# HGRN2 decays in a hybrid diffusion backbone: running products of the gates in place of exponentials of summed logarithms

## The chip, the cores and the metric

The kernel runs on one core of one Trainium2 chip. The metric is device time in microseconds (us) of one execution; the median of three runs is given, lower is better. Matmuls run on TensorE (PE; its weight loads are PEld), elementwise work on VectorE (DVE), ScalarE (ACT) and GpSimd (POOL); SyncE (SP) starts the transfers. Each engine works off its own instructions in a fixed order and waits on semaphores for the others.

## What is computed

Two layers, each a mixer with four head groups (HGRN2, SSD, RG-LRU, retention; all in both directions) and a ConvFFN. One sample, 256 context and 512 latent tokens, 1024 features, float32. The part that changes is the HGRN2 group: four heads of 128 channels, two directions, a gate per token and channel.

```python
log_f = jnp.logaddexp(jnp.log(jnp.maximum(lb_s, LB_FLOOR)), jnp.log1p(-lb_s) + jax.nn.log_sigmoid(u))
k_a = (1.0 - lb_s) * jax.nn.sigmoid(-u)
...
def step(S, inp):          # gla_chunk_scan, one chunk of tokens
    b = jnp.cumsum(lc, axis=1)
    rel = masked_decay(mask, b[:, :, None] - b[:, None, :])
    scores = jnp.sum(qc[:, :, None] * kc[:, None] * rel, axis=-1)
    y = (jnp.einsum("btsh,bshv->bthv", scores, vc)
         + jnp.einsum("bthk,bhkv->bthv", qc * jnp.exp(b), S))
    b_last = b[:, -1]
    S = (jnp.exp(b_last)[..., None] * S
         + jnp.einsum("bshk,bshv->bhkv", kc * jnp.exp(b_last[:, None] - b), vc))
```

The score of a query at t and a key at s is weighted, channel by channel, with the product of the gates between them.

## The kernel before

Every projection is a float32 product made of three matmuls with split operands (`proj_T`, line 303, columns on the partitions; `proj_N`, line 320, tokens on the partitions). A unit of weights `wr` comes by DMA; `Weights` (line 287 and 288) splits it: ACT casts the high part `wh`, then DVE makes the low part `wl` as a difference. A group of 24 matmuls fills one PSUM tile `pp` (there are three), which ACT or DVE empties.

Beside the projections run the mixers of the head groups, in the order `C0 C1 A0 A1 BC B0 B1 D0 D1` (A is HGRN2; the digit is a half of 256 channels, two heads). `interleave` (line 1291) emits steps of both by estimated times, and a scheduler, which models durations of its own, then sets each engine's order. Casts and evacuations carry a high priority there, so that what stands in an engine's row ahead of a cast is what the scheduler thought would be over in time.

HGRN2 works on chunks of 128 tokens, six of them, in two parts of three (`p`; in layer 1 part 0 scores only one chunk).

- `prepA` (line 547), once per half: sigmoids on ACT (556, 557), gate bounds on DVE (561 to 564), two logarithms per head and direction on ACT (568, 569), their sum on POOL (573), and a scan on DVE that sums the logs along each chunk (574). The result stays in `E`.
- `mixA_head` (line 583), once per head: scores at eight levels. Level -1 takes equal tokens; level `lev` takes pairs of adjacent blocks of m = 2^lev tokens, and weights both sides with the decay to the border between the blocks. For each level and part DVE and POOL take differences of the sums (657 to 660), ACT takes their exponential `g` (661), DVE and POOL multiply queries and keys with it into `lv` (664, 667), and PE makes the block products (672), which DVE merges under a mask (678). Every level starts again from `E`, so levels do not depend on one another.
- Beside the levels, `states` takes keys decayed to the chunk's end (595 to 601), whose products with the values go through `state_chain`; lines 690 to 695 make queries decayed from the chunk's start, and line 705 adds all up.

## Time and profile before

| | |
|---|---|
| device time, median of 3 runs | 2704.52 us |
| lowest, highest | 2702.71, 2708.85 us |
| profiled execution: span from first to last instruction | 2706.8 us |
| instructions in it | 42271 |
| mean granted TensorE clock | 0.967 |
| DVE, ACT, POOL busy | 1810.4, 1138.2, 1027.8 us |

For the profiled execution no device time of its own is listed beside the span; the span lies 2.3 us above the median and inside the range of the three runs. Busy times of different engines overlap, so they do not add up to the span. A matmul's length in the trace is its stay in a pipeline; the pace is the distance between starts.

### The profile page before, as it was taken

What the parts mean: (1) busy time and instruction counts of PE and PEld (TensorE: products, weight loads), DVE (VectorE), ACT (ScalarE), POOL (GpSimd) and SP (SyncE); (2) the same over time, 40 slices, a digit from 0 to 9 for tenths busy, and PEclk for the clock granted to TensorE, in tenths of its full rate; (3) what the DMA queues carried; (4) which work ended last, traced back from release to release, by engine and by line L of the source; (5) the groups of instructions that cost most, each with busy time, mean ns of one, the idle gap of its engine ahead of it and who ended that gap; (6) DMA issues with size and microseconds to landing.
All of it is one profiled execution on the core that took longest, in us unless ns stands there. A gap on an engine that the chain in (4) does not pass through costs nothing.

```text
span 2706.8 us, 42271 instructions
## 1 busy us (share of the span) xinstructions
PE 2512.5 (93%) x15910; PEld 2175.9 (80%) x15910; DVE 1810.4 (67%) x3573; ACT 1138.2 (42%) x2118; POOL 1027.8 (38%) x1327
## 2 busy tenths in 40 slices
PE   6878989998999989999999989799989999899997
PEld 4877888888997877878888878687789987788885
DVE  3898879887674673434344677988887767644457
ACT  3864464532332153322322267656442342543332
POOL 0346736366341760000001574564646436400006
PEclk9989999999999999999999989899999999899999
DMA  7134421233265264442222422212132264323333
GB/s 256 52 111 153 132 75 55 64 121 98 65 210 174 72 194 149 139 133 79 63 63 74 129 87 61 73 54 85 33 115 77 82 222 136 110 91 97 97 113 106
DMA packets 201596, 291.08 MB, mean 108 GB/s; under 512 B 15568, under 2 KB 145200, under 8 KB 201392
## 3 DMA queue, kind: packets, MB, share of 16 engines
q1 hardware_dynamic: 201392, 288.37, 34.3%
q8 instruction: 126, 2.06, 0.3%
q14 instruction: 78, 0.64, 0.1%
HBM read 256.73 MB, written 31.59 MB: 107 GB/s over the span
## 4 chain that ended last, share of the span: by engine, by line
PE 55%; DVE 24%; POOL 7%; DMA 6%; issue 4%; ACT 3%; SPq 0%; DVEq 0%; POOLq 0%; ACTq 0%
PE pp L313 25%; PE pp L1201 13%; PE pp L330 8%; DVE wl L288 3%; PE pp L1245 2%; DVE lv__t L664 1%; DVE g__t L658 1%; DVE g__t L657 1%; DVE lv__t L667 1%; PE ada__pm L383 1%; DVE E__t L574 1%; POOL S__t L1223 1%; DMA aB__t<-rowsd 1%; POOL aff__t L1281 1%; POOL aff__t L1282 1%
## 5 line engine op out<-in xcount | busy, mean ns | idle before, releaser
L313 PE MATMUL pp<-uh,wl 128*128 128x512 f32 (+2 forms) x1952 | 684.5, 351 | 21.4 <-DVE wl L288 13.7
L313 PE MATMUL pp<-ul,wh 128*128 128x512 f32 (+2 forms) x1952 | 681.5, 350 | 15.3 <-DVE ul L499 15.3
L313 PE MATMUL pp<-uh,wh 128*128 128x512 f32 (+2 forms) x1952 | 676.5, 347 | 0.0
L288 DVE TENSOR_TENSOR wl<-wr,wh 128x512 fp32r<-128x512 f32 (+1 forms) x552 | 432.9, 798 | 163.7 <-ACT wh L287 163.0
L287 ACT CAST wh<-wr 128x512 fp32r<-128x512 f32 (+1 forms) x552 | 337.2, 621 | 454.5 <-PE pp L1201 216.6
L313 PEld LDWEIGHTS pp<-uh,wl 128*128 128x128 f32 x1952 | 376.4, 193 | 69.2 <-DVE wl L288 15.2
L313 PEld LDWEIGHTS pp<-ul,wh 128*128 128x128 f32 x1952 | 377.1, 193 | 62.4 <-DVE ul L499 18.1
L313 PEld LDWEIGHTS pp<-uh,wh 128*128 128x128 f32 x1952 | 377.0, 193 | 42.2 <-issue 4.5
L330 PE MATMUL pp<-wl,uh 128*128 128x256 f32 (+1 forms) x1216 | 357.5, 294 | 16.3 <-DVE wl L288 16.2
L330 PE MATMUL pp<-wh,ul 128*128 128x256 f32 (+1 forms) x1216 | 361.1, 297 | 5.4 <-DVE gst__t L1416 3.3
L330 PE MATMUL pp<-wh,uh 128*128 128x256 f32 (+1 forms) x1216 | 353.1, 291 | 0.0
L330 PEld LDWEIGHTS pp<-wl,uh 128*128 128x128 f32 x1216 | 236.1, 194 | 21.5 <-DVE wl L288 17.3
L893 POOL MEMSET padF__t<- 128x1 f32 x44 | 4.3, 97 | 654.2 <-DVE gt__t L909 286.4
L330 PEld LDWEIGHTS pp<-wh,ul 128*128 128x128 f32 x1216 | 235.7, 194 | 10.1 <-DVE gst__t L1416 4.2
L330 PEld LDWEIGHTS pp<-wh,uh 128*128 128x128 f32 x1216 | 236.1, 194 | 1.5 <-issue 0.4
L1201 PE MATMUL pp<-wh,ccl__t 128*128 128x512 f32 x440 | 173.5, 398 | 2.1 <-DVE gst__t L1416 2.1
L1201 PE MATMUL pp<-wh,cch__t 128*128 128x512 f32 x440 | 174.0, 396 | 0.0
L1201 PE MATMUL pp<-wl,cch__t 128*128 128x512 f32 x440 | 173.7, 395 | 0.0
L1210 DVE TENSOR_TENSOR S__t<-pp,S__t 128x384 f32<-128x384 f32 (+1 forms) x240 | 89.7, 417 | 124.0 <-PE pp L1201 123.4
L909 DVE SCALAR_TENSOR_TENSOR cva__t<-padF__t,PT,cva__t 128x769 f32<-128x769 f32 (+1 forms) x44 | 42.0, 954 | 136.2 <-ACT cva__t L905 136.0
L1218 POOL TENSOR_TENSOR S__t<-S__t,bc__t 128x384 f32<-128x384 f32 (+1 forms) x60 | 60.2, 1016 | 172.0 <-DVE S__t L1210 170.1
L661 ACT ACTIVATE g__t<-g__t 128x768 f32<-128x768 f32 (+1 forms) x112 | 81.2, 736 | 93.4 <-DVE g__t L658 51.0
(359 smaller groups left out, 4911.4 us busy)
## 6 DMA issues: line engine op xcount, KB each, us to landing
wr<-w_in_dram SPq DMA_DIRECT2D x112, 512.0 KB, 4.0
wr<-ffn_w_in_dram SPq DMA_DIRECT2D x88, 512.0 KB, 3.6
wr<-ada_w_dram SPq DMA_DIRECT2D x80, 512.0 KB, 4.2
wr<-ffn_w_out_dram SPq DMA_DIRECT2D x44, 512.0 KB, 3.8
wr<-w_out_dram SPq DMA_DIRECT2D x32, 512.0 KB, 5.0
aB__t<-rowsd SPq DMA_DIRECT2D x40, 256.0 KB, 3.9
adw__t<-ada_w_dram SPq DMA_DIRECT2D x32, 256.0 KB, 5.3
hres<-aff__t SPq DMA_DIRECT2D x32, 192.0 KB, 1.9
```

The source lines that it names most:

```text
L287: A.copy(hi[:, :m], rq)
L288: V.tensor_tensor(out=lo[:, :m], in0=rq, in1=hi[:, :m].bitcast(F32), op=SUB)
L313: PE.matmul(ps[:, :t1 - t0], a[:, cs], b[k // 4][:, k % 4, t0:t1], start=n == 0, stop=n == 23)
L330: PE.matmul(ps[:, :nn], a[k // 4][:, k % 4, ts], b, start=n == 0, stop=n == 23)
L383: PE.matmul(ps[32 * (j0 + j):32 * (j0 + j) + 32, :256], condT[:, k, :], raw[x][:, j * 256:(j + 1) * 256], start=k == 0, stop=k == 7)
L574: V.tensor_tensor_scan(out=e, data0=st["scan"], data1=e, initial=0.0, op0=MULT, op1=ADD)
L661: A.activation(g[:, :2 * N], g[:, :2 * N], AF.Exp)
L909: V.scalar_tensor_tensor(out=o[:, lo:hi], in0=pad[:, lo + j:hi + j], scalar=w(j), in1=acc[:, lo:hi], op0=MULT, op1=ADD)
L1201: PE.matmul(ps, a[:, ts], b, start=n == 0, stop=n == 3 * kt - 1)
L1210: V.tensor_tensor(out=o, in0=src, in1=o, op=ADD)
L1218: G.tensor_tensor(out=o, in0=o, in1=gcols(r, lo, hi), op=MULT)
L1245: PE.matmul(ps, a[:, ts], b, start=n == 0, stop=n == 3 * kt - 1)
```

## The change

The gates themselves are kept, no logarithms. For each head and part one tile `f2` holds the gates of both directions, `k2` the keys of both. `prepA` keeps the sigmoids and the bounds (line 564, 565 of the changed kernel) and loses the logarithms, their sum, the scan and the scan's constant. In `mixA_head`, queries `Q` start as q times the gate (`begin`, line 629); at each level `scores` gathers the keys of both directions by an ACT copy into `kl` (595), or takes the tiles as they are at level 6, and lets the queries be read with strides by PE (609). Then `grow` makes the next level in place: POOL multiplies the half of the keys that lie ahead of a border with the product of the gates of the neighbouring block (643), DVE does the same to the queries (646) and halves the table of block products `tot` (649). After level 6, keys and queries are decayed over the whole chunk, and `states` and the output take them as they are. Both parts of a head now go through the levels together. Comments also go, and with them line numbers move.

```diff
 def projA(l, u, hf, dtr, st):
-        E = [[t3(f"E{d}{h}") for h in range(2)] for d in range(2)]
+        f2 = {(h, p): t3(f"f{h}{p}") for h in range(2) for p in range(2)}
...
-                A.copy(v3(E[d][ct], 129)[:, t0 // 128:t1 // 128, 1:129], v3(ps[:, :t1 - t0], 128))
+                A.copy(f2[ct, t0 // PW][:, d * PW:(d + 1) * PW], ps[:, :t1 - t0])
...
 def prepA(st, prm):
-            V.tensor_scalar(out=E1[x], in0=E1[x], scalar1=c1, scalar2=fl, op0=MULT, op1=ADD)
-            V.tensor_scalar(out=v3(l2[x], 128), in0=E1[x], scalar1=2.0 ** 60, scalar2=1.0, op0=MULT, op1=MIN)
-            V.tensor_scalar(out=E1[x], in0=E1[x], scalar1=2.0 ** -60, scalar2=None, op0=MAX)
-            V.tensor_scalar(out=k[x][:, :768], in0=k[x][:, :768], scalar1=c1, scalar2=None, op0=MULT)
...
-                A.activation(l2[x], l2[x], AF.Ln)
-                last = A.activation(E1[x], E1[x], AF.Ln)
...
-            G.tensor_tensor(out=E1[x], in0=E1[x], in1=v3(l2[x], 128), op=ADD)
-            V.tensor_tensor_scan(out=e, data0=st["scan"], data1=e, initial=0.0, op0=MULT, op1=ADD)
+                f, k = st["f2"][h, p][:, ds], st["k2"][h, p][:, ds]
+                V.tensor_scalar(out=f, in0=f, scalar1=c1, scalar2=fl, op0=MULT, op1=ADD)
+                V.tensor_scalar(out=k, in0=k, scalar1=c1, scalar2=None, op0=MULT)
...
 def mixA_head(st, prm, y, h):
...
+            elif lev < 6:
+                ks = t3("kl")
+                A.copy(ks[:, :N], strided(K[p], chs[p][0] % 3 * 128, [[2 * m, N // (2 * m)], [PW + m, 2], [1, m]]))
...
+                    elif lev < 6:
+                        ql = strided(Q[p], qc, [[2 * m, 32 // m], [N + m, 2], [1, m]])
+                    else:
+                        kl = K[p][:, hs * PW + kc:hs * PW + kc + 64]
+                        qo = j * 128 + 64 + N if hs == 0 else j * 128
+                        ql = Q[p][:, qo:qo + 64]
+                    PE.matmul(sc[64 * hs:64 * hs + 64, j * 64:(j + 1) * 64], kl, ql, start=True, stop=True)
...
+        def begin(p):
+            V.tensor_tensor(out=v3(Q[p][:, :2 * N], N), in0=q[:, None, t0:t0 + N].to_broadcast([128, 2, N]),
+                            in1=strided(f, fo + PW, [[-PW, 2], [1, N]]), op=MULT)
+        def grow(p, lev):
...
+            G.tensor_tensor(out=strided(K[p], 0, [[2 * m, nk], [PW + m, 2], [1, m]]),
+                            in0=strided(K[p], 0, [[2 * m, nk], [PW + m, 2], [1, m]]),
+                            in1=strided(t, off + 1, [[2, nk], [step - 1, 2], [0, m]]), op=MULT)
+            V.tensor_tensor(out=strided(Q[p], 0, [[2 * m, nq], [N + m, 2], [1, m]]),
+                            in0=strided(Q[p], 0, [[2 * m, nq], [N + m, 2], [1, m]]),
+                            in1=strided(t, off + step + b0 + 1, [[2, nq], [-step - 1, 2], [0, m]]), op=MULT)
+            V.tensor_tensor(out=strided(tn, noff, [[nk, 2], [1, nk]]), in0=strided(t, off, [[step, 2], [2, nk]]),
+                            in1=strided(t, off + 1, [[step, 2], [2, nk]]), op=MULT)
+            tot[p] = (tn, noff, nk)
...
+        for lev in range(-1, 7):
+            for p in range(2):
+                if lev == 0:
+                    begin(p)
+                scores(p, lev)
+                if lev >= 0:
+                    grow(p, lev)
+                yield 1.8
+        for p in range(2):
+            states(p)
+            yield 2.0
```

`strided(t, off, dims)` is a view of a tile from column `off` on, with a step and a count for each dimension. The tile of 774 columns holds forward data in columns 0 to 383 and backward data in 384 to 767, so at m = 1 the pattern of `grow` goes back and forth between the two with every element.

The change moves instructions on all engines; the orders below show three places. ACT, layer 0, second half, around the evacuations of the query projection, before (`E` the summed logs, `dec` and `kt` the exponentials for the states, `q` the queries that leave PSUM):

```order
L591 ACTIVATE decA__ss_4098<-E__t_2732 128x6
L597 ACTIVATE kt__t_4101<-kt__t_4101 128x384
L533 COPY q__t_3782<-pp 128x384
L591 ACTIVATE decA__ss_4098<-E__t_2734 128x6
L598 ACTIVATE kt__t_4101<-E__t_2734 128x384
L591 ACTIVATE decA__ss_4773<-E__t_2733 128x6
L533 COPY q__t_3783<-pp 128x384
L287 CAST wh<-wr 128x512
```

Each exponential that reads `E` comes after a scan of line 574, and the cast of the next weights stands behind it. In the changed kernel ACT has, a little earlier in the same half:

```order
L530 COPY f__t_2693<-pp 128x384
L556 ACTIVATE k__t_3691<-f__t_2693 128x768
L557 ACTIVATE f__t_2693<-f__t_2693 128x768
L595 COPY kl__t_3874<-k__t_3690 128x384
L595 COPY kl__t_3860<-k__t_3691 128x384
L595 COPY kl__t_3927<-k__t_3690 128x384
L595 COPY kl__t_3887<-k__t_3691 128x384
L530 COPY f__t_2694<-pp 128x384
L595 COPY kl__t_3953<-k__t_3690 128x384
L556 ACTIVATE k__t_3692<-f__t_2694 128x768
L284 CAST wh<-wr 128x512
```

No scan and no logarithm is left ahead of a cast; copies of keys, each behind a growth step on POOL, stand there now. The same in layer 0, first half, around the four evacuations of the queries, changed kernel:

```order
L535 COPY q__t_1718<-pp 128x384
L284 CAST wh<-wr 128x512
L595 COPY kl__t_2133<-k__t_1870 128x384
L595 COPY kl__t_2181<-k__t_1871 128x384
L595 COPY kl__t_2194<-k__t_1870 128x384
L535 COPY q__t_1718<-pp 128x384
L595 COPY kl__t_2243<-k__t_1871 128x384
L595 COPY kl__t_2256<-k__t_1870 128x384
L535 COPY q__t_1719<-pp 128x384
L595 COPY kl__t_2328<-k__t_1871 128x384
L284 CAST wh<-wr 128x512
L595 COPY kl__t_2341<-k__t_1870 128x384
```

The fourth evacuation comes right behind. Between the first and the fourth PE passes three groups of 24 matmuls, and ACT seven copies. POOL, layer 0, second half, before and then in the changed kernel (`ks` are the keys of level -1):

```order
L643 TENSOR_TENSOR ks__t_4089<-k__t_3910,k__t_3911 128x384
L505 TENSOR_TENSOR rs__ss_3674<-rs__ss_3674,pw 128x3
L573 TENSOR_TENSOR E__t_2732<-E__t_2732,l__t_3914 128x6x128
L573 TENSOR_TENSOR E__t_2734<-E__t_2734,l__t_3915 128x6x128
L659 TENSOR_TENSOR g__t_4108<-E__t_2732 128x192
L573 TENSOR_TENSOR E__t_2733<-E__t_2733,l__t_3916 128x6x128
L659 TENSOR_TENSOR g__t_4148<-E__t_2732 128x96x2
```

```order
L590 TENSOR_TENSOR ks__t_3795<-k__t_3690 128x384
L643 TENSOR_TENSOR k__t_3690<-k__t_3690,f__t_2692 128x192x2
L590 TENSOR_TENSOR ks__t_3805<-k__t_3691 128x384
L643 TENSOR_TENSOR k__t_3690<-k__t_3690,tot__t_3826 128x96x2x2
L643 TENSOR_TENSOR k__t_3691<-k__t_3691,f__t_2693 128x192x2
L643 TENSOR_TENSOR k__t_3690<-k__t_3690,tot__t_3826 128x48x2x4
L502 TENSOR_TENSOR rs__ss_3376<-rs__ss_3376,pw 128x3
```

Three instructions on a quarter of the data per level have become one on all 768 columns, each behind the one before it on the same tile. PE's matmuls are the same in number and shape in both orders.

## Rows read from the trace of the kernel before

**Rows 1.** The page, part 1: busy us (share of the span) xinstructions.

```profile
PE 2512.5 (93%) x15910; PEld 2175.9 (80%) x15910; DVE 1810.4 (67%) x3573; ACT 1138.2 (42%) x2118; POOL 1027.8 (38%) x1327
```

**Rows 2.** Windows: stretch, length, busy PE PEld DVE ACT POOL, clock, DMA, GB/s.

```profile
150.00:545.00 395.00, 360.35 (x2887) 319.95 (x2886) 342.31 (x615) 209.62 (x382) 219.35 (x282) 0.94 0.33 103
1690.00:2005.00 315.00, 278.38 (x1975) 243.38 (x1974) 272.68 (x567) 175.90 (x349) 175.23 (x275) 0.95 0.22 65
```

**Rows 3.** Waits of PE, whole span: who waited for whom, us in total, times, longest.

```profile
PE sc__pm L672 <- DVE lv__t L667: 18.1, 12, 4.0
...
PE pp L330 <- DVE wl L288: 16.2, 4, 8.7
...
PE pp L313 <- DVE wl L288: 13.7, 5, 7.4
```

**Rows 4.** Timeline, layer 0, first half: start, length, instruction [idle before <-releaser].

```profile
192.95 1.58 ACT L569 ACTIVATE E__t<-E__t 128x768 f32<-128x768 f32 x2 [3.50 <-DVE E__t L563]
...
194.44 0.61 ACT L287 CAST wh<-wr 128x512 fp32r<-128x512 f32 x1
...
198.38 0.94 DVE L288 TENSOR_TENSOR wl<-wr,wh 128x512 fp32r<-128x512 f32 x1
...
199.35 0.34 SPq L377 DMA_DIRECT2D wr<-ada_w_dram  x1
...
203.32 1.08 PE L383 MATMUL ada__pm<-wr,condT 128*32 128x256 f32 x8 [7.75 <-DMA wr<-ada_w_dram]
```

**Rows 5.** Timeline, layer 0, second half.

```profile
381.82 4.21 DVE L574 TENSOR_TENSOR_SCAN E__t<-scan__t,E__t 128x774 f32<-128x774 f32 x2
...
384.41 0.21 ACT L591 ACTIVATE decA__ss<-E__t 128x6 f32<-128x6 f32 x1 [5.49 <-DVE E__t L574]
...
384.89 0.62 ACT L287 CAST wh<-wr 128x512 fp32r<-128x512 f32 x1
...
386.68 0.69 PE L313 MATMUL pp<-uh,wl 128*128 128x384 f32 x1 [7.39 <-DVE wl L288]
```

**Rows 6.** Timeline, layer 1, first and (last two rows) second half.

```profile
1726.29 0.84 ACT L568 ACTIVATE l__t<-l__t 128x768 f32<-128x768 f32 x1 [6.01 <-DVE l__t L562]
...
1730.19 0.58 PE L330 MATMUL pp<-wl,uh 128*128 128x256 f32 x1 [8.70 <-DVE wl L288]
...
1862.71 0.21 ACT L591 ACTIVATE decA__ss<-E__t 128x6 f32<-128x6 f32 x1 [4.34 <-DVE E__t L574]
...
1867.26 0.79 PE L313 MATMUL pp<-uh,wl 128*128 128x512 f32 x1 [4.50 <-DVE wl L288]
```

**Rows 7.** Windows behind those four gaps; columns as in rows 2.

```profile
197.50:207.80 10.30, 4.48 (x19) 3.67 (x20) 10.30 (x12) 3.85 (x7) 7.10 (x5) 0.52 0.48 135
382.00:392.40 10.40, 5.72 (x18) 5.73 (x19) 10.40 (x13) 5.34 (x11) 5.08 (x7) 0.51 0.19 51
1723.60:1733.90 10.30, 3.71 (x17) 3.71 (x18) 10.30 (x11) 7.38 (x10) 6.80 (x5) 0.50 0.19 52
1867.00:1870.40 3.40, 3.14 (x7) 2.48 (x8) 3.40 (x7) 1.83 (x6) 0.84 (x1) 0.50 0.56 155
```

**Rows 8.** Groups by line and shape: xcount | busy us, mean ns | idle before.

```profile
L574 DVE TENSOR_TENSOR_SCAN E__t<-scan__t,E__t 128x774 f32<-128x774 f32 x16 | 34.4, 2152 | 2.7 <-POOL E__t L573 2.7
...
L664 DVE TENSOR_TENSOR lv__t<-q__t,g__t 128x384 f32<-128x384 f32 x84 | 63.6, 760 | 5.6 <-ACT g__t L661 3.8 <-PE yA__pm L705 1.5 <-DMA gsp0A<-gst__t 0.2
...
L661 ACT ACTIVATE g__t<-g__t 128x768 f32<-128x768 f32 x84 | 69.7, 843 | 74.0 <-DVE g__t L658 39.3 <-POOL g__t L660 24.2 <-DVE rs__ss L720 4.7
...
L528 ACT COPY E__t<-pp 128x384 f32<-128x384 f32 x32 | 15.1, 474 | 16.5 <-PE pp L313 16.2
```

**Rows 9.** Tile E, POOL: xcount: ns min/median/max, first and last start, shapes.

```profile
L573 POOL TENSOR_TENSOR E__t<-E__t,l__t x16: 1683/1998/3150, 186.7 to 1859.2; 128x768 f32<-128x768 f32 x16
```

**Rows 10.** Timeline, PE: a first and a last projection matmul, 21 apart.

```profile
189.71 0.34 PE L313 MATMUL pp<-uh,wl 128*128 128x384 f32 x1
...
193.39 0.34 PE L313 MATMUL pp<-uh,wl 128*128 128x384 f32 x1
```

More of the change, by code (lines that the diff above doesn't have):

```diff
@@ L162, in host_constants @@
     ramps = np.concatenate([r1, r2, rampf, rampb, cols], axis=1)
-    scan = np.ones((128, NCH, 129), f)
-    scan[:, :, 0] = 0.0
     masks = np.zeros((128, 6, 64), f)
@@ L181, in host_constants @@
         "ramps": np.ascontiguousarray(ramps),
-        "scan": np.ascontiguousarray(scan.reshape(128, T3W)),
         "masks": np.ascontiguousarray(masks.reshape(128, 384)),
@@ L505, in rsqrt, with strided @@
         G.tensor_tensor(out=x, in0=x, in1=pw.to_broadcast([128, n]), op=ALU.pow)
+    PW = 384
+    def strided(t, off, dims):
+        base = t[:, 0:1]
+        return bass.AP(base.tensor, base.offset + off, [list(base.ap[0])] + [list(d) for d in dims])
     def projA(l, u, hf, dtr, st):
@@ L549, in prepA @@
         l = st["l"]
[L550 to L553 removed]
+        hp = [(h, p) for h in range(2) for p in range(2)]
+        st["k2"] = {x: t3("k2") for x in hp}
         with HP():
[L555 to L557 removed]
@@ L566, in prepA @@
-        with HP(), after(last):
-            for x in hd:
-                A.activation(l2[x], l2[x], AF.Ln)
-                last = A.activation(E1[x], E1[x], AF.Ln)
-        st["last"] = last
-        for x in hd:
-            e = st["E"][x[1]][x[0]]
-            G.tensor_tensor(out=E1[x], in0=E1[x], in1=v3(l2[x], 128), op=ADD)
-            V.tensor_tensor_scan(out=e, data0=st["scan"], data1=e, initial=0.0, op0=MULT, op1=ADD)
-            yield 2.0
-        for h in range(2):
-            st["k", h] = [k[h, d] for d in range(2)]
+            for x in hp:
+                A.activation(st["k2"][x][:, :768], st["f2"][x][:, :768], AF.Sigmoid, scale=-1.0)
+                A.activation(st["f2"][x][:, :768], st["f2"][x][:, :768], AF.Sigmoid)
@@ L579, in mixA_head @@
+        for h, p in hp:
+            for d in range(2):
+                j = d * 4 + 2 * st["hf"] + h
+                ds = slice(d * PW, (d + 1) * PW)
+                c1, fl = prm["c1"][:, l, j:j + 1], prm["fl"][:, l, j:j + 1]
+                f, k = st["f2"][h, p][:, ds], st["k2"][h, p][:, ds]
+                V.tensor_scalar(out=f, in0=f, scalar1=c1, scalar2=fl, op0=MULT, op1=ADD)
+                V.tensor_scalar(out=k, in0=k, scalar1=c1, scalar2=None, op0=MULT)
+            yield 1.5
     def mixA_head(st, prm, y, h):
@@ new lines, in states @@
+        def states(p):
+            kt = K[p][:, :768].rearrange("p (d c t) -> p d c t", d=2, c=3)
+            ktn = t3("ktn")[:, :768].rearrange("p (d c t) -> p d c t", d=2, c=3)
+            for d in range(2):
+                pt = pm("ktT")
+                for c in range(3):
+                    PE.transpose(pt[:, c * 128:(c + 1) * 128], kt[:, d, c, :], ident)
+                A.copy(ktn[:, d], v3(pt[:, :384], 128))
+            for d in range(2):
+                last = 5 if d == 0 else 2
+                ps = pm("dl")
+                for c in range(3):
+                    if 3 * p + c == last:
+                        continue
+                    PE.matmul(ps[:, c * 128:(c + 1) * 128], ktn[:, d, c, :],
+                              v3(i[p][:, :768], 256)[:, c, h * 128:(h + 1) * 128], start=True, stop=True)
+                dt_ = t3("dls")
+                A.copy(dt_[:, :384], ps[:, :384]) if last // 3 != p else A.copy(dt_[:, :256], ps[:, :256])
+                dl[d, p] = dt_
@@ new lines, in mixA_head, with dec @@
+        for lev in range(-1, 7):
+            for p in range(2):
+                if lev == 0:
+                    begin(p)
[3 more added lines that the diff above has]
+                yield 1.8
+        for p in range(2):
+            states(p)
+            yield 2.0
+        for d in range(2):
+            Sin.append(v3(t3(f"S{d}")[:, :768], 128))
+            def dec(c):
+                t, off, step = tot[c // 3]
+                return t[:, off + d * step + c % 3:off + d * step + c % 3 + 1]
+            state_chain(Sin[d], d, lambda c: dl[d, c // 3][:, (c % 3) * 128:(c % 3 + 1) * 128], dec)
@@ L1437, in mA @@
         def mA(hf):
-            if hf == 0:
-                X["scan"] = t3("scan")
-                SY.dma_start(out=X["scan"], in_=I["scan"])
-            X["A", hf]["scan"] = X["scan"]
             y = [t3(f"yA{p}") for p in range(2)]
```

182 lines of the change are left out of this document (54 added, 128 removed).

## Prediction, made before the changed kernel ran

> **What bounds the kernel now.** I read the page's busy times first: PE is busy for 93% of the span, 2512.5 us, no other engine for more than 67% [rows 1]. PE's matmuls are the same in number and shape after the change, so what it can win is time in which PE waits, and time in which PE runs at the lower clock because it had waited. Then I cut the span into stretches. HGRN2 lies in 150 to 545 us and 1690 to 2005 us; there PE is idle for 34.7 us (395.00 less 360.35) and 36.6 us, at a granted clock of 0.94 and 0.95 [rows 2]. That is the purse: some 70 us, shared with groups B and C.
>
> Third, the waits of PE. The score matmuls wait 18.1 us for queries and keys that DVE has multiplied, in 12 pieces; projection matmuls wait for the low part of their weights, 16.2 and 13.7 us, with single waits of 8.7 and 7.4 us [rows 3]. Last, the timeline around the longest ones. All four begin in `prepA` or right behind it, once for each half of each layer, and have one cause. ACT takes its instructions in order, and a cast of weights stands behind a logarithm or an exponential that waits for DVE. In layer 0 ACT idles 3.50 us for the bounds on DVE, casts at 194.44, DVE makes the low part at 198.38, only then is the buffer free, the transfer issued at 199.35, and PE has idled 7.75 us [rows 4]. In the second half DVE is in two scans of 4.21 us together; the exponential of the chunk decays waits 5.49 us for them, the cast follows at 384.89, PE has idled 7.39 us [rows 5]. In layer 1 a logarithm waits 6.01 us for DVE and PE idles 8.70 us; in its second half the chunk decay waits 4.34 us for a scan and PE idles 4.50 us [rows 6]. Together 7.75 + 7.39 + 8.70 + 4.50 = 28.3 us.
>
> Behind each gap the granted clock is 0.50 to 0.52, that is 1.2 GHz instead of 2.4, after PE had stood still [rows 7]. In those windows PE is busy 4.48 + 5.72 + 3.71 + 3.14 = 17.1 us, half of which, 8.5 us, full clock would give back.
>
> **The change, part by part.**
>
> *Logarithms, sum, scan and chunk decays go.* With them goes every instruction for which ACT waited in the four gaps, and 34.4 us of scans on DVE [rows 8]. At stake are 28.3 + 8.5 = 36.8 us. The casts now stand behind sigmoids, which wait for PE alone, and behind copies of keys (below). In the windows of the first and third gap DVE has no idle time at all [rows 7], since group C's chain runs there too; some lateness of the low parts stays. I keep a quarter: **-27.6 us** (bounds -18.4, half kept, and -36.8).
>
> *Levels.* For each of 112 pairs of level and part, two differences, two products and one exponential become one product of all queries, a small table product and a copy of keys. The removed exponential took 843 ns, a product of 384 took 760 ns on DVE, the added copy has half of the exponential's elements and should take about the 474 ns of an ACT copy of 384 [rows 8]. For the 768 queries I bound DVE's product by one and two of those 760 ns, and the table, which has as many elements over all seven levels together, by the same once per part; both lie beside projection matmuls. But the next level's scores wait for the in-place product, which waits for the present level's scores, where before levels were independent. So of the 18.1 us at the scores [rows 3] I take half off: **-9.1 us** (bounds 0 and -18.1). PE now reads queries with strides. At the pace of 21 matmuls in 3.68 us, 0.175 us each of 384 columns [rows 10], 64 columns take 0.03 us; the 80 matmuls of m = 1, if they take double or four times that, cost up to 5 to 7 us. Nothing in the trace reads so; I take 0, as it would be one level of eight.
>
> *Key growth on POOL.* Each level multiplies all 768 columns. The nearest row is POOL's sum of 768, median 1998 ns, 1683 to 3150 [rows 9]. A head has 14 of them and two sums of half that size: 14 x 2.0 + 2 x 1.0 = 30 us in one chain, mostly ahead of PE. What stands behind it is ACT: seven copies, each behind a growth, stand among four evacuations in layer 0. Seven growths take 14.0 us, a product of group C's beside them 2.0, while PE passes three groups of 24 matmuls, 3 x 24 x 0.175 = 12.6 us: evacuations and casts come up to 3.4 us late. In the second half three growths and a sum, 7.0 us, meet one group of 4.2 us: 2.8 us late. With three PSUM tiles PE can go on for two groups, 8.4 us, before a late evacuation stops it, but not past a late weight. Eight heads at 0 to about 3.1 us give 0 to 25 us. I take **+5 us**, nearer to the low end because of that slack. The Trainium skill (GPSIMD Engine Reference, 3.1 Elementwise — side-by-side cycle accounting) says that GpSimd needs about 2.6 cycles for an element of a two-input product, and gives 4497 ns for 2048 elements, about half the speed of VectorE; scaled, that is an estimate of 1.69 us for 768. By that figure the growths would keep pace and this term would be 0; the shortest of the row agrees, the median is 18% longer, and I go by the median.
>
> *The rest.* Halved bounds on DVE, two transfers of the scan's constant, and the products at lines 595 to 601 and 690 to 695 go; they lie beside PE's work, cost nothing now, and I count no gain. `states` moves behind the last level. What is late next if the gaps close are the score products on DVE and, in layer 1, group B, which the new order starts slightly later among PE's matmuls.
>
> *Sum:* -27.6 - 9.1 + 5 = -31.7 us against the span of 2706.8: 2675.1 us. The median lies 2.3 us under that span, so **2673 us**. A measurement of this kernel tells changes of about 0.2%, 5.4 us, from none.
>
> **The rivals.**
>
> *All of it comes.* No quarter stays, scores never wait, POOL keeps ahead: -36.8 - 18.1 = -54.9, 2650 us. For it: every engine beside PE has less to do. Against: the levels are now a chain.
>
> *ACT behind POOL in place of ACT behind DVE.* Casts stand behind key copies; half of the gaps stay (-18.4), four heads pay 3.1 us (+12.4), scores wait as before: -6, 2699 us. For it: ACT already waits for POOL at the exponential, 24.2 us in that group [rows 8]. Against: a copy waits for one growth, the old wait was for a queue of scans.
>
> *Slower: growth is the bound.* PE has, by the new order, a group of 24 matmuls for each of eight levels and about two more for states and outputs: ten times 4.2, 42 us a head. POOL's chain is longer from (42 - 2) / 14 = 2.86 us per growth on. At 3.15 us, the longest of the row [rows 9], it takes 46.1 us: 4.1 x 8 = 33 us of PE waits at the scores, and half of the gaps stay: +33 - 18.4 = +14.4, 2719 us. For it: at m = 1 the pattern jumps 387 columns and back with every element, and contention with DVE already stretches the row from 1683 to 3150. Against: the median, 1998. The Trainium skill (SBUF — State Buffer, Door 1: The DMA port swizzle) states that consecutive accesses want two hits in a 16-byte line, and that each access that crosses to a new line pays a penalty; here m = 1 has one hit, m = 2 two, and larger m full lines. By that rule the first level or two alone would be slow, on POOL, DVE, ACT and PE; no row here shows such a pattern.
>
> That the change does not do what it says can be left out: the new order has no logarithm or scan in HGRN2.
>
> **How the numbers follow.** The forecast has 0.60, its own range 2655 to 2693 (the bounds of its terms). All of it 0.12, ACT behind POOL 0.13, growth as the bound 0.15. Faster by over 0.2%: 0.58 of the forecast, 0.12, and 0.06 of the second rival, 0.76. Within 0.2%: 0.02 and 0.07, 0.09. Slower: 0.15. The range 2648 to 2708 leaves out the slower rival and a quarter of the first, 0.18.
>
> **What would show it.** Right: no PE wait above 4 us for low parts in HGRN2's stretches, their clock at 0.97 or more, a growth near 2.0 us, score waits near 9 us. Wrong: waits of ACT's key copies for POOL of tens of us with casts behind them; growths of 3 us, above all at m = 1; score waits above 20 us; or new gaps in group B, which I have not priced.

## The result, and the profile after

The changed kernel takes 2636.62 us (median of 4 runs, 2634.04 to 2640.76) against 2705.26 us before in the same comparison (2702.71 to 2708.85): a ratio of 0.9738, 95% interval 0.9718 to 0.9757. It is faster, as forecast, but by 68.6 us, where the prediction had 31.7 and its range ended at 2648. The profiled span fell from 2706.8 to 2632.2 us, the mean granted clock rose from 0.967 to 0.975.

The page of the changed kernel, busy time by engine, answers to [rows 1]:

```profile
PE 2485.0 (94%) x15910; PEld 2155.3 (82%) x15910; DVE 1630.3 (62%) x3301; ACT 1040.4 (40%) x1978; POOL 873.2 (33%) x1023
```

PE has the same 15910 matmuls and is busy for 27.5 us less, for the most part because it ran more of them at full clock (below). DVE lost 180 us, POOL 155.

The windows of HGRN2's stretches in the changed kernel, cut at the same places of the program as [rows 2]:

```profile
150.00:506.00 356.00, 344.10 (x2870) 307.73 (x2870) 247.42 (x485) 158.78 (x317) 130.36 (x135) 0.98 0.36 112
1650.00:1934.00 284.00, 268.97 (x2006) 237.44 (x2005) 203.00 (x429) 128.74 (x277) 106.56 (x124) 0.98 0.24 73
```

The two stretches shrank from 710 to 640 us, so nearly the whole gain lies in them. PE's idle time there fell from 34.7 + 36.6 to 11.9 + 15.0 us, by 44.4. Added up by the kind of matmul that waited (pauses under 0.15 us left out), it fell from 45.8 to 22.6 us at projections, from 22.2 to 2.6 us at scores and from 3.1 to 1.6 us elsewhere. Most of the rest is the clock: cutting the stretches into pieces of 2 us and adding up, over the pieces, PE's busy time times the part of full clock that was not granted gives 29.9 us before and 10.5 after, 19.4 us won. Some 6 us of the 70 are left without an account.

PE's waits in the changed kernel, over the whole span, answer to [rows 3]:

```profile
PE pp L310 <- DVE wl L285: 10.0, 3, 9.0
...
PE pp L327 <- DVE wl L285: 8.3, 2, 5.0
...
PE sc__pm L609 <- DVE q__t L646: 0.9, 2, 0.8
```

The scores waited 18.1 us for DVE's products, and now 0.9. The waits for low parts fell from 29.9 to 18.3 us, and half of those is one gap of 9.01 us in layer 1, at a matmul for which PE did not wait before. Of the prediction's four gaps two are gone; at the matmuls of the first and the third PE still waits 5.44 us (7.75 before) and 3.28 us (8.70). The timeline around the gap of 9.01 us (start, length, instruction, idle before it):

```profile
1664.05 2.08 POOL L643 TENSOR_TENSOR k__t<-k__t,f__t 128x384 f32<-128x384 f32 x1 [0.84 <-DVE f__t L564]
1664.37 0.60 ACT L284 CAST wh<-wr 128x512 fp32r<-128x512 f32 x1
1664.61 1.73 DVE L565 TENSOR_SCALAR k__t<-k__t,c 128x384 f32<-128x384 f32 x1
...
1667.13 0.41 DVE L565 TENSOR_SCALAR k__t<-k__t,c 128x384 f32<-128x384 f32 x1
1667.28 1.91 POOL L1127 TENSOR_TENSOR cg__t<-cg__t,cw__t 128x768 f32<-128x768 f32 x1 [1.16 <-DVE cw__t L1126]
1667.46 2.15 DVE L649 TENSOR_TENSOR tot__t<-f__t 128x384 f32<-128x384 f32 x1
...
1669.23 0.68 ACT L595 COPY kl__t<-k__t 128x384 f32<-128x384 f32 x1 [3.00 <-POOL cg__t L1127]
1669.82 0.61 ACT L284 CAST wh<-wr 128x512 fp32r<-128x512 f32 x1
...
1671.30 2.01 POOL L643 TENSOR_TENSOR k__t<-k__t,f__t 128x384 f32<-128x384 f32 x1 [0.84 <-DVE f__t L564]
1671.86 1.66 DVE L649 TENSOR_TENSOR tot__t<-tot__t 128x192 f32<-128x192 f32 x1
...
1674.10 0.68 DVE L285 TENSOR_TENSOR wl<-wr,wh 128x512 fp32r<-128x512 f32 x1
...
1674.84 0.79 PE L310 MATMUL pp<-uh,wl 128*128 128x512 f32 x1 [9.01 <-DVE wl L285]
```

Casts and low parts are equal in number, and taken in order the low part at 1674.10 belongs to the cast at 1664.37, which was over 9 us earlier. In between DVE is never idle: it works off group C's chain, the bounds and the new table products. Three of these take 1.73, 2.15 and 1.66 us beside products on POOL; the same shapes take 0.41 us at 1667.13, and 0.64 and 0.35 us on average in keys_dve, a run below with less on POOL. So by an estimate from these rows about 4 us of this gap is DVE standing still beside POOL, and the rest its order of work. A later cast, at 1669.82, does stand behind a key copy that waits for POOL, the picture of the prediction's second rival, but PE does not wait for it here.

The costs of the new levels (groups by line and shape):

```profile
L643 POOL TENSOR_TENSOR k__t<-k__t,tot__t 128x384 f32<-128x384 f32 x96 | 108.9, 1145 | 92.5 <-ACT kl__t L595 58.2 <-PE sc__pm L609 29.3 <-DVE tot__t L649 3.7
L643 POOL TENSOR_TENSOR k__t<-k__t,f__t 128x384 f32<-128x384 f32 x16 | 28.6, 1789 | 21.1 <-ACT kl__t L595 17.5 <-DVE f__t L564 3.0 <-DVE mv__ss L713 0.4
...
L646 DVE TENSOR_TENSOR q__t<-q__t,tot__t 128x384 f32<-128x384 f32 x72 | 48.4, 675 | 4.0 <-PE sc__pm L609 3.9
...
L595 ACT COPY kl__t<-k__t 128x384 f32<-128x384 f32 x72 | 39.6, 554 | 67.3 <-POOL k__t L643 30.9 <-POOL cg__t L1127 9.6 <-DVE S__t L546 5.5
```

A growth has 384 elements, not the 768 that the prediction and the section on the change give it: the pattern `[[2 * m, nk], [PW + m, 2], [1, m]]` takes one block of every two in each direction. It costs 1.15 us on average on POOL (1.79 at the first level), and POOL often waits before it, for ACT's copies and for PE.

### The profile page after: what moved, and what is told of

It reads as the page before. It is cut to its first block, busy times and chain, and to the rows that moved or that the text cites. A ratio compares the mean times of both kernels' runs of the same rounds, so it can differ in the third digit from the quotient of the medians.

```text
span 2632.2 us, 41479 instructions
## 1 busy us (share of the span) xinstructions
PE 2485.0 (94%) x15910; PEld 2155.3 (82%) x15910; DVE 1630.3 (62%) x3301; ACT 1040.4 (40%) x1978; POOL 873.2 (33%) x1023
## 5 line engine op out<-in xcount | busy, mean ns | idle before, releaser
L285 DVE TENSOR_TENSOR wl<-wr,wh 128x512 fp32r<-128x512 f32 (+1 forms) x552 | 422.0, 778 | 196.8 <-ACT wh L284 196.1
L643 POOL TENSOR_TENSOR k__t<-k__t,tot__t 128x384 f32<-128x384 f32 x96 | 108.9, 1145 | 92.5 <-ACT kl__t L595 58.2
```

The costliest lines, as they stand in the source:

```text
L285: V.tensor_tensor(out=lo[:, :m], in0=rq, in1=hi[:, :m].bitcast(F32), op=SUB)
L643: G.tensor_tensor(out=strided(K[p], 0, [[2 * m, nk], [PW + m, 2], [1, m]]), in0=strided(K[p], 0, [[2 * m, nk], [PW + m, 2], [1, m]]), in1= ...
```

## The experiments

Two theories stood after this. One: the prediction's causes were right and only its deductions (a quarter of the gaps kept, half of the score waits, 5 us for the growth) too cautious. The other: something was won that no term had. The first four runs take the change apart.

**prep_back: logarithms and scans put back beside the new levels.**

```diff
+ lg = {x: (t3("lge"), t3("lgl")) for x in hp}
...
+ V.tensor_scalar(out=l2[:, :768], in0=st["f2"][h, p][:, :768], scalar1=2.0 ** 60, scalar2=1.0, op0=MULT, op1=MIN)
+ V.tensor_scalar(out=e[:, :768], in0=st["f2"][h, p][:, :768], scalar1=2.0 ** -60, scalar2=None, op0=MAX)
...
+ A.activation(l2[:, :768], l2[:, :768], AF.Ln)
+ last = A.activation(e[:, :768], e[:, :768], AF.Ln)
...
+ G.tensor_tensor(out=e[:, :768], in0=e[:, :768], in1=l2[:, :768], op=ADD)
+ V.tensor_tensor_scan(out=e[:, :768], data0=st["f2"][x][:, :768], data1=e[:, :768], initial=0.0, op0=MULT, op1=ADD)
...
+ A.activation(dcs[:, p, :], v3(st["lge"][h, p][:, :768], 128)[:, :, 127], AF.Exp)
```

> The changed kernel with the logarithms, their bounds, the sums, the scans and the exponentials of the chunk decays put back in prepA, all into scratch tiles that nothing else reads; levels stay products. Theory (the four gaps are made by ACT's logarithms and exponentials that wait for DVE while casts of weights stand behind them): PE stands still again for 5 to 9 us behind prepA in most of the four halves, and the clock falls behind each; at the prediction's 28.3 us of gaps and 8.5 us of clock, up to the 19 us of clock that the trace of the changed kernel shows regained, the time is 2665 to 2684 us. Rival (the gaps closed because DVE has less to do in the levels, so that the scans now find room): less than 15 us come back, 2652 us or below.

Measured 2691.79 us, ratio 0.9944 (0.9928 to 0.996): 55 us come back, more than the theory's upper end, and the rival falls.

**logs_out: the kernel before without them.**

```diff
- A.activation(l2[x], l2[x], AF.Ln)
- last = A.activation(E1[x], E1[x], AF.Ln)
...
- G.tensor_tensor(out=E1[x], in0=E1[x], in1=v3(l2[x], 128), op=ADD)
- V.tensor_tensor_scan(out=e, data0=st["scan"], data1=e, initial=0.0, op0=MULT, op1=ADD)
```

> The kernel before with the logarithms, their bounds, the sums and the scans left out (the gates themselves stand where the summed logarithms stood, so the output is not the reference's); the levels stay exponentials of differences. Theory (gaps belong to prepA): 28 to 37 us are won, with a larger share of the clock up to 50: 2655 to 2677 us, the four gaps of 7.75, 7.39, 8.70 and 4.50 us are gone, and the score matmuls still wait about 18 us for products on DVE. Rival (the levels load DVE and ACT so much that the gaps stay): less than 15 us, 2690 us or more.

Measured 2687.00 us, ratio 0.9937 (0.9917 to 0.9957): 19.5 us won, between the two theories. Two of the four gaps are gone; at the first PE still waits 5.0 us, and around the third 4.1 and 2.1 us. In the stretches the idle time at projections falls from 45.8 to 23.6 us, at scores it stays (22.2 and 22.4). The largest of the scores' waits over the whole span:

```profile
PE sc__pm L663 <- DVE lv__t L658: 15.2, 8, 3.0
```

So 14.7 us for the levels alone (prep_back against before) and 19.5 for the logarithms alone make 34, close to the prediction's 31.7, though neither part is the prediction's (4.1 and 27.6). Both together make 70. The surplus of some 35 us is what had to be found.

**keys_twice and level1_split: the growth's size, and its first level.**

```diff
+ gd = t3("gd")
+ G.tensor_tensor(out=strided(gd, 0, [[2 * m, nk], [PW + m, 2], [1, m]]),
+                 in0=strided(K[p], 0, [[2 * m, nk], [PW + m, 2], [1, m]]),
+                 in1=strided(t, off + 1, [[2, nk], [step - 1, 2], [0, m]]), op=MULT)
  G.tensor_tensor(out=strided(K[p], 0, [[2 * m, nk], [PW + m, 2], [1, m]]),
```

> The changed kernel with each growth of keys done twice on POOL, first into a scratch tile, then in place, so that a level pays for 768 elements, as the prediction had priced it, in two instructions of together about 2.3 us. Theory (the halved growth, 384 and not 768 elements, is why the levels cost nothing): the scores wait about 9 us again and casts behind key copies add about 5, so 10 to 18 us more, 2646 to 2655 us. Rival (the chain of growths has slack even at this size): within 4 us of 2636.6. Rival (growth as the bound): 33 us more or worse, 2669 us and above, with waits of PE for keys above 20 us.

Measured 2654.59 us, ratio 0.9805 (0.9789 to 0.9821): 18 us more, at the theory's end. Why, the run alone doesn't tell; keys_memset below does.

```diff
+ if lev == 0:
+     for d in range(2):
+         G.tensor_tensor(out=strided(K[p], d * (PW + 1), [[2, nk]]), in0=strided(K[p], d * (PW + 1), [[2, nk]]),
+                         in1=strided(t, off + 1 + d * (step - 1), [[2, nk]]), op=MULT)
+     for d in range(2):
+         V.tensor_tensor(out=strided(Q[p], d * (N + 1), [[2, nq]]), in0=strided(Q[p], d * (N + 1), [[2, nq]]),
+                         in1=strided(t, off + step + b0 + 1 - d * (step + 1), [[2, nq]]), op=MULT)
```

> The changed kernel with the growth of the first level (m = 1) split by direction: two products of 192 elements at every second column on POOL and on DVE, in place of one product of 384 whose elements jump 385 columns and back. The Trainium skill (SBUF - State Buffer, Door 1: The DMA port swizzle) has a penalty where consecutive accesses hit a 16-byte line only once; every second column hits it twice. By that rule each half goes at the pace of the other levels: about 0.45 to 0.6 us on POOL, together about 1.0 in place of 1.7, and on DVE about 0.35 each, together 0.7 in place of 1.1. Rival (any step other than 1 is slow): the halves together take 1.6 us or more on POOL and 1.1 on DVE. The time in both: within 4 us of 2636.6, since the first level is one of seven and not what PE waits for.

Measured 2631.77 us, ratio 0.9724 (0.9709 to 0.9738), 4.9 us under the changed kernel, where 4 at most was expected; the intervals of the two overlap, so no gain is shown. The tile's row for POOL, ns shortest/median/longest:

```profile
L645 POOL TENSOR_TENSOR k__t<-k__t,f__t x32: 683/732/1414, 175.5 to 1859.7; 128x192 f32<-128x192 f32 x32
```

Two halves take 1.46 us by the median, against 1.72 for the whole product (shortest 1.56): on POOL neither theory's price. On DVE a half of the queries takes 649 ns on average here, beside POOL's products, and 396 ns in keys_dve_split below, without them; a half of the keys takes 351 ns there. That is 0.70 to 0.79 us for two halves, near the first theory's price.

**order_only, ln_back, scan_back: what in prepA costs the 55 us.**

```diff
- yield 1.5
+ yield 2.0
+ for _ in range(4):
+     yield 2.0
```

> The changed kernel with the costs that prep_back gives prepA in the hand-set interleaving (four steps of 1.5 become eight of 2.0) and none of its instructions: the same order of the program's parts, so the control of prep_back. Theory (the 55 us of prep_back are its logarithms and scans): within 6 us of 2636.6. Rival (the order alone costs it, since the levels then meet other projections): 2660 us or more.

Measured 2645.98 us, ratio 0.9779 (0.9749 to 0.9809): about 9 us of prep_back are the order of the steps alone, somewhat above the theory's 6; the instructions cost 45.8. The windows of order_only and then of prep_back, cut alike:

```profile
150.00:506.00 356.00, 342.90 (x2865) 305.20 (x2865) 240.10 (x471) 152.72 (x306) 127.33 (x133) 0.98 0.36 111
1663.00:1958.00 295.00, 284.52 (x2160) 254.04 (x2158) 207.10 (x448) 135.43 (x290) 104.84 (x126) 0.99 0.27 80
```

```profile
150.00:522.50 372.50, 348.04 (x2866) 308.81 (x2865) 269.85 (x498) 169.10 (x332) 147.02 (x141) 0.97 0.35 107
1669.50:2001.50 332.00, 302.64 (x2201) 270.42 (x2200) 246.64 (x478) 155.65 (x328) 132.25 (x137) 0.95 0.24 72
```

PE idles 53.8 us in place of 23.6, which is 30.2 more. It is chance that this lies near the 28.3 us of the prediction's four gaps: 17.8 of it stand at projections and 13.9 at scores, and elsewhere PE idles 1.2 us less. What it loses at the low clock, added up over pieces as above, is 22.7 in place of 7.1, 15.6 more, where the prediction had 8.5. Together that is 45.8 us, as much as the medians differ; the two profiled spans lie only 41.2 us apart, so some of it is won back outside the stretches.

ln_back takes from prep_back the line of the scan:

```diff
- V.tensor_tensor_scan(out=e[:, :768], data0=st["f2"][x][:, :768], data1=e[:, :768], initial=0.0, op0=MULT, op1=ADD)
```

> prep_back without its scans: bounds on DVE, sums on POOL, logarithms and the exponentials of the decays on ACT stay, all on scratch. Theory of the prediction (ACT stands at a logarithm that waits for DVE's bounds, casts behind it): at least half of the 55 us stays, 2664 us or more, with PE waits for low parts or weights above 4 us behind prepA. Rival (the scans fill DVE, and the low parts, which DVE makes, come late whatever ACT does): less than a third stays, 2655 us or less.

Measured 2673.59 us, ratio 0.9874 (0.9848 to 0.9901). scan_back takes away ACT's part:

```diff
- A.activation(l2[:, :768], l2[:, :768], AF.Ln)
- last = A.activation(e[:, :768], e[:, :768], AF.Ln)
...
- A.activation(dcs[:, p, :], v3(st["lge"][h, p][:, :768], 128)[:, :, 127], AF.Exp)
```

> prep_back without logarithms and exponentials of decays: bounds and scans on DVE and sums on POOL stay, on scratch; nothing is added on ACT. Theory of the prediction: less than a third of the 55 us stays, 2655 us or less, as no cast stands behind an instruction that waits for DVE. Rival (DVE's load): at least half stays, 2664 us or more. If both this and ln_back stay above 2655, the two add up to the 55 us or each is enough to break the cover.

Measured 2678.40 us, ratio 0.9896 (0.9874 to 0.9919). Above order_only the logarithms cost 27.6 us without a scan and the scans 32.4 without a logarithm, 45.8 both. Each alone does more than half of the harm. With nothing added on ACT, the bounds and scans on DVE and the sums on POOL are enough, so the prediction's cause (ACT stands, casts behind it) is not the only one. But both runs keep the bounds and the sums, so what these cost is in both figures: neither run shows what ACT's logarithms or DVE's scans do alone.

**keys_dve: the growth of keys on DVE.**

```diff
- G.tensor_tensor(out=strided(K[p], 0, [[2 * m, nk], [PW + m, 2], [1, m]]),
+ V.tensor_tensor(out=strided(K[p], 0, [[2 * m, nk], [PW + m, 2], [1, m]]),
```

> The changed kernel with the growth of keys on DVE in place of POOL: 112 products of 384 elements at about 0.55 us (0.87 and more at m = 1) in place of 0.85 to 1.72, so DVE is busy for some 65 to 75 us more and POOL for 137 less. keys_twice showed that POOL's chain still counts: doubling it cost 18 us. Theory (the chain of growths is partly on the path): a shorter chain wins up to 8 us, 2628 to 2637 us. Rival (DVE's load is what counts, 70 % in these stretches, and low parts of weights queue behind the growths): 5 to 25 us lost, 2642 to 2662 us.

Measured 2625.47 us, ratio 0.9697 (0.9673 to 0.9721): 11 us won, somewhat beyond the theory; the rival falls. The groups of the growth, and the windows of this kernel:

```profile
L643 DVE TENSOR_TENSOR k__t<-k__t,tot__t 128x384 f32<-128x384 f32 x96 | 53.5, 562 | 20.8 <-ACT kl__t L595 13.5 <-PE sc__pm L609 7.0
...
L643 DVE TENSOR_TENSOR k__t<-k__t,f__t 128x384 f32<-128x384 f32 x16 | 13.8, 874 | 0.3 <-ACT kl__t L595 0.2
```

```profile
150.00:499.50 349.50, 341.06 (x2868) 306.41 (x2867) 244.37 (x538) 153.26 (x306) 69.76 (x78) 0.99 0.37 114
1657.00:1934.00 277.00, 267.09 (x2015) 237.78 (x2014) 200.45 (x485) 132.52 (x282) 40.94 (x68) 0.99 0.25 76
```

DVE took on 67.3 us of products and is busy in the stretches for 444.8 us, where it was 450.4. Its other instructions became shorter by about as much: the 912 that fall into the changed kernel's stretches keep it busy for 449.7 us there and for 393.4 us here.

**keys_memset: is it POOL's chain, or that POOL reads?**

```diff
+ gd = t3("gd")
+ G.memset(gd, 0.0)
+ G.memset(gd[:, :384], 0.0)
  G.tensor_tensor(out=strided(K[p], 0, [[2 * m, nk], [PW + m, 2], [1, m]]),
```

> The changed kernel with two fills of a scratch tile (774 and 384 columns) on POOL ahead of each growth of keys: by the profile's rows of smaller fills (99 ns for 2 columns, 311 ns for 256) about 1.15 us together, as long as the second product of keys_twice (1.02 us median), but without reading or multiplying anything. Theory (keys_twice paid 18 us because DVE and POOL get in each other's way where both read SBUF, which stretches DVE's own products): most of the 18 us is not paid, 2645 us or less, and DVE's busy time in the two stretches stays near 451 us. Rival (keys_twice paid for its longer chain of growths): 2649 us or more, as in keys_twice, whatever DVE's busy time.

Measured 2632.49 us, ratio 0.9729 (0.9712 to 0.9746): nothing paid. The windows of keys_memset, then of keys_twice:

```profile
150.00:503.60 353.60, 343.21 (x2862) 305.37 (x2862) 244.56 (x477) 154.42 (x308) 181.54 (x245) 0.98 0.37 113
1652.50:1934.50 282.00, 265.18 (x1965) 235.23 (x1964) 201.67 (x417) 127.30 (x274) 158.72 (x235) 0.96 0.23 69
```

```profile
150.00:518.00 368.00, 347.92 (x2875) 310.18 (x2874) 268.79 (x481) 155.21 (x312) 190.92 (x189) 0.98 0.35 109
1661.00:1966.00 305.00, 275.24 (x2013) 243.13 (x2013) 230.56 (x430) 129.22 (x279) 173.10 (x182) 0.96 0.23 69
```

POOL is busy for 340 us with the fills and 364 with the second product. DVE's windows, 446 and 499 us, do not hold quite the same instructions (894 and 911). Over the same 912 instructions as above DVE is busy for 457 us with the fills and 497 with the second product, where the changed kernel has 450. So some 130 us more on POOL cost nothing by themselves.

The single instructions of keys_memset show the same, as the time that DVE takes beyond the shortest instruction of the same form (mean in ns, number of instructions in brackets; all operands in SBUF):

| what POOL does meanwhile | DVE: two input tensors | DVE: one (`tensor_scalar`) |
|---|---|---|
| nothing | 18 (929) | 9 (249) |
| fills alone | 52 (127) | 525 (12) |
| instructions that read, alone | 382 (438) | 342 (80) |

A POOL instruction that reads SBUF makes DVE's instructions with two inputs longer; one that only writes hardly does. That is a rule of the Trainium skill (SBUF — State Buffer, Who interferes with whom): a DVE instruction with two SBUF inputs contends with a GpSimd instruction that reads SBUF, not with one that only writes, and the loser waits. These two runs agree, with 40 us of DVE's time and 22 of the kernel's between them. Instructions with one input are lengthened too, by fills perhaps as well (12 cases).

**before_dve and logs_out_dve: the same in the kernel before.**

```diff
- G.tensor_tensor(out=bl1(gk)[:, :, :, 0, :], in0=fb, in1=f1[:, :, :, 0, :], op=SUB)
- G.tensor_tensor(out=bl1(gk)[:, :, :, 1, :], in0=b0[:, :, :, 1, :], in1=bb, op=SUB)
+ V.tensor_tensor(out=bl1(gk)[:, :, :, 0, :], in0=fb, in1=f1[:, :, :, 0, :], op=SUB)
+ V.tensor_tensor(out=bl1(gk)[:, :, :, 1, :], in0=b0[:, :, :, 1, :], in1=bb, op=SUB)
...
- eng = V if w else G
- eng.tensor_tensor(out=bl1(kl)[:, :, :, w, :], in0=bl1(k[w][:, tk])[:, :, :, w, :],
+ V.tensor_tensor(out=bl1(kl)[:, :, :, w, :], in0=bl1(k[w][:, tk])[:, :, :, w, :],
```

> The kernel before with the levels' work on POOL (two differences and one product for each pair of level and part, 192 elements each) moved to DVE: 336 instructions, some 90 to 120 us of DVE's time if each takes 0.27 to 0.35 us. DVE is busy for 618 of 713 us in the two stretches before. Theory of load (DVE's busy time is work): it then has more than the stretches hold, and the time rises by 20 us or more, 2726 us and above. Theory of getting in each other's way (a good part of DVE's 618 us is waiting for POOL): its busy time grows by less than half of the added work and the time stays within 15 us of 2706.

Measured 2690.06 us, ratio 0.9947 (0.9929 to 0.9965): DVE does 336 instructions more, and the kernel is 15.6 us faster. The theory of load falls; the 15 us of the other are just passed. Two of its groups (the first answers to L664 in [rows 8], at 760 ns; L658 took 585 ns before), and its windows:

```profile
L664 DVE TENSOR_TENSOR lv__t<-q__t,g__t 128x384 f32<-128x384 f32 x84 | 48.7, 580 | 2.2 <-ACT g__t L661 2.0
...
L658 DVE TENSOR_TENSOR g__t<-E__t 128x192 f32<-128x192 f32 x84 | 32.2, 384 | 0.0
```

```profile
150.00:531.00 381.00, 351.00 (x2847) 309.59 (x2846) 325.99 (x763) 207.70 (x378) 123.47 (x111) 0.96 0.33 102
1686.00:1981.00 295.00, 273.77 (x1965) 239.22 (x1964) 265.74 (x716) 183.25 (x351) 90.75 (x103) 0.96 0.22 66
```

This cut leaves out some 40 of DVE's instructions. Over the 1181 of [rows 2]'s stretches DVE was busy for 617 us before; over the same work and the 336 added instructions it is busy for 609. So a part of what [rows 2] and [rows 8] show as DVE's work was waiting for POOL.

> before_dve without logarithms, bounds, sums and scans, as in logs_out (the gates stand where the summed logarithms stood). Rival (the two add up): 15.5 us of before_dve and 19.5 of logs_out, 2671 us, give or take 5. Theory (POOL's work in the levels covered what the logarithms' removal gives): 35 us or more below before_dve, 2655 us or less.

The edit is before_dve's and logs_out's in one. Measured 2644.03 us, ratio 0.9774 (0.9758 to 0.9791): 46.0 us below before_dve, as the theory had it. With the old exponentials in place this is within 8 us of the changed kernel: most of the gain needs no products of gates, only the logarithms gone and POOL's share moved.

**prep_back_dve** (prep_back and keys_dve in one).

> prep_back with the growth of keys on DVE in place of POOL. Without logarithms and scans this is keys_dve, 2625.5 us, and the order of prep_back adds 9.4 (order_only), 2634.9. Theory (POOL's reading in the levels is what makes the logarithms and scans dear): less than 25 us above that, 2660 us or less. Rival (prepA costs its 45.8 us by itself, in the order of ACT and in DVE's time): 2675 to 2688 us.

Measured 2675.29 us, ratio 0.9891 (0.987 to 0.9912), as the rival had it: that POOL's reading in the levels makes the logarithms dear falls. What the logarithms and scans cost, in us, by the levels that stand beside them:

| levels | with them | without | they cost |
|---|---|---|---|
| differences, POOL's share on POOL (before) | 2706.5 | 2687.0 | 19.5 |
| differences, all on DVE | 2690.1 | 2644.0 | 46.0 |
| products, keys on POOL | 2691.8 | 2646.0 | 45.8 |
| products, keys on DVE | 2675.3 | 2634.9, an estimate: 2625.5 and order_only's 9.4 | 40 |

They cost 40 to 46 us in three cases of four. Only the old levels with POOL's 336 instructions in them hide 26 us of it. Where it hides, the traces show. PE's time in the stretches, in us, added up as in the section on the result:

| run | idle at projections | idle at scores | idle elsewhere | lost at the low clock |
|---|---|---|---|---|
| before | 45.8 | 22.2 | 3.1 | 29.9 |
| logs_out | 23.6 | 22.4 | 4.7 | 24.7 |
| before_dve | 38.6 | 10.0 | 2.4 | 19.5 |
| logs_out_dve | 16.1 | 4.8 | 2.4 | 9.3 |
| prep_back | 36.9 | 14.8 | 2.1 | 22.7 |
| order_only | 19.1 | 0.9 | 3.3 | 7.1 |

Without logarithms and scans the projections wait 18 to 23 us less, whichever levels stand beside. The scores gain nothing in the old kernel, where they still wait for products on DVE, and 5.2 and 13.9 us in the others; the clock gains 5.2 us in the old kernel, 10.2 and 15.6 in the others. So the surplus lies at the scores and in the clock.

**keys_dve_split, keys_dve_c, more_dve: how far it goes.** The first joins keys_dve and level1_split, all on DVE.

> keys_dve with the first level's products split by direction, as in level1_split, all on DVE: 16 growths of keys at 0.87 us and 16 of queries become 32 and 32 of about 0.35 us each, which is 5 us less on DVE. Theory (what counts is DVE's time and the chain): 0 to 5 us won on keys_dve, 2620 to 2626 us. Rival (the fixed cost of more instructions, or another order): 2 to 8 us lost, 2627 to 2633 us.

Measured 2623.80 us, ratio 0.9699 (0.9685 to 0.9714), not to be told from keys_dve. keys_dve_c moves two products of group C as well:

```diff
- G.tensor_tensor(out=g, in0=g, in1=cx[:, :T], op=MULT)
+ V.tensor_tensor(out=g, in0=g, in1=cx[:, :T], op=MULT)
...
- G.tensor_tensor(out=g, in0=g, in1=w, op=MULT)
+ V.tensor_tensor(out=g, in0=g, in1=w, op=MULT)
```

> keys_dve with the two gate products of group C's chain moved from POOL to DVE as well: 32 products of 768 columns of 1.9 us on POOL become 32 of about 0.95 us on DVE; 16 of each kind, half of them in HGRN2's stretches. Theory (POOL's reading is paid for by DVE as waiting, and the chain gets shorter): 0 to 12 us won, 2613 to 2626 us. Rival (DVE is at its limit in prepA, where group C's chain runs): 5 to 20 us lost, 2631 to 2646 us.

Measured 2604.25 us, ratio 0.9631 (0.9617 to 0.9646), the fastest kernel here, 101 us under the one before and 21 under keys_dve, where the theory had 12 at most. Its page:

```profile
PE 2470.8 (95%) x15910; PEld 2147.8 (83%) x15910; DVE 1630.5 (63%) x3445; ACT 1044.7 (40%) x1980; POOL 665.8 (26%) x879
```

DVE has 144 instructions more than in the changed kernel and the same busy time to 0.2 us. Group C's chain is shorter too, since each of the 32 products takes 0.95 us where it took 2.1 to 2.6; how much of the 21 us is that, no run shows.

> keys_dve_c with the first level split as in keys_dve_split and two more of POOL's steps on DVE: the sum of the keys of both directions (16 of 384 columns, 1.4 us on POOL) and the sum of group C's two directions (8, 1.9 us or more). Theory (what reads on POOL is paid for on DVE): 2 to 8 us won on keys_dve_c, 2596 to 2602 us. Rival (DVE becomes late where PE waits for it): 2 to 10 us lost, 2606 to 2614 us.

The edit adds `V` for `G` at the keys' sum and at the sum of group C's directions. Measured 2606.90 us, ratio 0.9630 (0.961 to 0.965): no different from keys_dve_c. Here moving work off POOL shows no further gain.

## Why the prediction was wrong in size

The sign and the place were right, the size was not. In the stretches PE's idle time fell by 23.2 us at projections, where three quarters of the four gaps are 21.2; by 19.6 at scores, where the prediction had 9.1; and by 1.5 elsewhere. The low clock cost 19.4 us less, where three quarters of 8.5 are 6.4. So the terms that failed are the clock, 13 us short, the scores, 10.5 short, and the 5 us for the growth, for which PE shows no wait; what it does cost is not what the prediction had in mind (below). About 11 us of the 74.6 by which the profiled spans differ have no account, half of them outside the stretches.

Along the runs the change falls into three steps: new levels, 2706.5 to 2691.8 (prep_back); logarithms and scans out, to 2646.0 (order_only); the steps of prepA at lower cost in the interleaving, to 2636.6. That is -14.7, -45.8 and -9.4, where the prediction's terms were -4.1 (-9.1 and +5), -27.6 and 0. In the other order the logarithms come first with -19.5 (logs_out), less than the prediction's 27.6, and the rest is -50.4. So no single price belongs to a term. The prediction priced them apart and added them, while the scores' waits and the loss at the low clock go in full only when both go, the logarithms and POOL's share in the levels.

- **"half of which, 8.5 us, full clock would give back": the clock is the step that failed most.** It was counted in the four windows of [rows 7] only. The stretches lost 29.9 us to the low clock before and 10.5 after. The bound should have come from the granted clock of the whole stretches in [rows 2], 0.94 and 0.95 over 710 us, and not from the four gaps.
- **"I keep a quarter"** held for the idle time, in part by luck. At the four gaps' matmuls 8.7 of 28.3 us stay; a new gap of 9.0 us came, and many smaller waits went. A quarter was kept because DVE had no idle time in those windows; the same DVE was full in part because it stood still beside POOL, as the gap of 9.01 us shows.
- **"Half off" for the scores' waits.** Nearly all went, 18.1 to 0.9 us. The prediction feared the new chain of levels. But these waits were put down to DVE's products, and DVE was waiting for POOL: with POOL's share moved, waits of the scores for these products fall to 4.7 us in the old kernel as well.
- **"Key growth on POOL, +5."** Mis-sized twice, in elements (384, not 768) and in kind. More time on POOL costs nothing by itself (keys_memset); what costs is that POOL reads beside DVE, 18 us for 132.5 us of it (keys_twice). By that the change should gain on POOL, off which it takes 154.6 us. [Rows 9] held the hint, 1683 to 3150 ns for one shape, and the prediction named contention as its cause, yet it priced it for POOL alone and not for DVE. Set against growths on DVE, those on POOL cost 11 us (keys_dve). The forecast's range kept the term at +5, between bounds of 0 and 25.
- **"The rest: I count no gain."** order_only shows about 9 us for the costs that set the order.
- **PE's strided queries, 0** (up to 5 to 7): of the right size. The matmuls of m = 1 take 253 ns by the median, those of m = 2 take 224 and all others 222; there are 160 of them, not 80, and 160 at 0.03 us are 5 us at most.
- **The rivals.** "All of it comes", 2650, was nearest and missed the clock. "ACT behind POOL" did not come true: the one long gap is DVE's work, stretched by POOL. "Growth is the bound" never came near its point: 1.79 us on average at the worst level against 2.86. The rule that it leaned on, the Trainium skill's two hits in a 16-byte line (SBUF — State Buffer, Door 1: The DMA port swizzle), is borne out on DVE: 874 ns at m = 1 against 562 at all other levels. On POOL it is not, in that form: the shortest growth falls step by step, 1559 ns at m = 1, 1185 at m = 2, 992 at m = 4, 839 at m = 64. It did not matter for the time.
- **What was to show it:** clock at 0.97 or more, yes (0.98); growth near 2.0, no; score waits near 9, no; no wait above 4 us for low parts in these stretches, missed once (9.0; the 5.44 us at the first gap are a wait for a weight's transfer); no new gap in group B, as hoped.

Open is how the 45.8 us split between ACT's order, DVE's time and POOL's sums: ln_back and scan_back cost 28 and 32 us, share the bounds and the sums, and do not add up. That the meeting of POOL and DVE is the whole of the levels' 14.7 us is likely from before_dve's 15.6, not shown.

## What to carry to other kernels

A busy DVE is not a working DVE: before pricing what a change takes off it, compare the shortest and the mean of one shape, and ask which POOL instruction reads SBUF at that time. Moving two-input work from POOL to DVE can shorten DVE's own time. And terms that act through the same engine do not add up: price them together as well as alone, and take the low clock from the whole stretch, not from the gaps.

## What was not expected of the hardware

DVE's product of 384 elements took 760 ns on average beside POOL's differences and 580 ns without them, a difference of 192 elements 585 and 384 ns. 112 products moved from POOL to DVE left DVE's busy time in the stretches at 445 us, from 450; 336 instructions in the kernel before lowered it from 617 to 609. Over the same 912 instructions DVE was busy for 450 us in the changed kernel, 457 with fills added on POOL (340 us busy in all) and 497 with products added (364). DVE's scalings of one input are lengthened beside POOL as well: 1.73 us in place of 0.41 in the gap shown above.
